# Longer lists of used rows in the second layer, and value rows copied next to their weights

## The chip, the cores and the metric

The kernel runs on one core of one Trainium2 chip. The metric is the device time of one execution in microseconds. Three runs of the kernel before took 1823.28, 1824.83 and 1824.98 us; the median is 1824.83 us. The change is judged by its median against that one.

## The reference

A decoder trunk of two layers over 256 tokens with 1024 features. Layer 0 mixes tokens by a state-space scan, layer 1 by causal attention. Behind each stands a product-key expert mixer (PEER), a layer norm, and a gated embedding. The change is in the expert mixer of layer 1:

```python
def block(xb):                                    # 128 tokens
    q = (xb @ w_q).reshape(128, 8, 2, 128)
    s = einsum('thcd,hcnd->thcn', q, sub_keys)
    v1, i1 = top_k(s[:, :, 0], 16)
    v2, i2 = top_k(s[:, :, 1], 16)
    cand = v1[..., :, None] + v2[..., None, :]
    best, pos = top_k(cand, 16)                   # 16 of 256 for each of 8 heads
    expert = take(i1 * 128 + i2, pos)
    gate = softmax(best)
    act = gelu(einsum('td,thkd->thk', xb, u[expert]))
    return einsum('thk,thkd->td', gate * act, v[expert])
```

There are 16384 experts, each with a row of u and a row of v (1024 floats). A token uses 8 x 16 of them.

## The kernel before

**Tiling.** The 256 tokens are two blocks of 128. The experts are 128 columns of 128 rows: row p of column e is expert 128 e + p. `peer(i)` does the expert mixer of layer i in four steps.

1. Queries, scores and the top-k lists ("route"), from lines 782 and 867 on.
2. `expert_in(e)` computes all 128 columns' products with u, whether used or not: 16 matmuls a column, accumulated in f32 from a high and a low part. Between the columns, `pick`, `spread` and `finish` make the gate of every (expert, token) and multiply it in. At the end `act[:, e, :]` holds the weight of every row of column e for all 256 tokens (columns from `MANY` = 92 on are in `high`). A matmul in line 993 counts beside it, per block of tokens, which rows of the first `MANY` columns are used at all.
3. `listing()` makes lists from that. A row of the first 92 columns that both token blocks use is of class "both"; one that only the first or the second uses is "one" or "two". Each class has places for `CAPS` = (37, 22, 22) groups of 128 rows, `GROUPS` = 81 in all. Prefix sums (`sums`, `ranks`), a 0/1 matrix per 8 columns (`place`) and a sort by `max` and `match_replace` (`order`) yield, for group s, the 128 row numbers: `picked["v"]` into v, `picked["w"]` into the table of weights. If a class overflows, a general loop over all columns runs behind a branch; else it is jumped over.
4. The sum over v. The last 36 columns are "dense": `expert_load` loads the 128 rows of v with SP and `expert_out` does 12 matmuls. The 92 others are done by groups: the weights were written to the DRAM tables `w_d` (256 tokens) and `a_d` (the first 128) by `keep` on ACT's DMA queue, 8 columns and 128 tokens a time. `fetched(s)` lets POOL (GpSimd) gather for a group first its 128 rows of weights, then its 128 rows of v. `group_load` splits both into a high and a low part (ACT casts, DVE subtracts), and `group_out` does 12 matmuls for "both" and 6 for the other classes.

**Order.** Engines work in order, and the code writes the order out by hand: `emit` sorts steps by a fraction of the stretch. Behind the last `expert_in` come six dense columns (`LEAD`), then the "one" groups with 13 dense columns between them (`MIX`), then the "both" and "two" groups (called inner) with the other dense columns but three and the loads of the gate's weights (`gate_load`). The last three dense columns (`LATER`) and the last two groups (`TAIL`) stand at the end, around the final layer norm. `issue_after` marks tie a step's instructions to the ones of the step before.

**Buffers.** In the "one" stretch, of three groups two gather v into the tiles `early` and one into the ring `raw` of four, which dense columns use too. In the inner stretch six tiles `raws` are used in turn. Split values go to the ring `hl` of four.

## Time and profile before

| what | us or count |
|---|---|
| profiled execution | 1825.7 |
| its span (first to last instruction) | 1823.9 |
| median of the runs | 1824.83 |
| second layer: attention and its start | about 929 to 1072 |
| second layer: queries and scores | about 1072 to 1131 |
| second layer: expert columns, gating | about 1131 to 1498 |
| second layer: lists built | about 1498 to 1532 |
| second layer: "one" groups | about 1532 to 1602 (POOL) |
| second layer: inner groups | about 1602 to 1784 |
| gathers in the second layer (L1189) | 162, 1531.88 to 1777.35 |

How to read it: the profile's first part gives the busy time and number of instructions of each engine; PE is the matrix engine, PEld its weight loads. In the second part each digit is the busy share in one of 40 slices of 45.6 us. In a table of stretches every engine has its busy time and number of instructions, then come the granted clock of PE, the share of the 16 DMA engines and GB/s. A row of the time order has the start, the duration and, in brackets, the idle time ahead with what ended it. `acc` are the sums, `hl` a split chunk, `w` a split weight tile.

### The profile page before, as it was taken

To read this page: it belongs to the slowest core of one execution; us is meant where nothing else is said; L and a number is where in the kernel's file an instruction comes from. 1 tells how busy PE (TensorE), PEld (TensorE's weight loads), DVE (VectorE), ACT (ScalarE), POOL (GpSimd) and SP (SyncE) were. 2 spreads that over 40 slices of the span, in tenths; PEclk is the share of its full clock that TensorE was granted. 3 is DMA by queue.
4 is the path that set the end of the run, shared out by engine and by line. 5 is a ranking of instruction groups with operands and counts; after the bars stand their busy time and mean duration, and the time that the engine had idled before them with its cause. 6 is when DMAs were issued, how large, how long until landed. Compare 5 with 4: busy or idle time off the path is not lost.

```text
span 1823.9 us, 31779 instructions
## 1 busy us (share of the span) xinstructions
PE 1806.1 (99%) x11152; PEld 1543.8 (85%) x11152; DVE 1493.5 (82%) x2948; ACT 1155.7 (63%) x2326; POOL 629.4 (35%) x608
## 2 busy tenths in 40 slices
PE   8999999999999999999999999999999999999999
PEld 7998888888888888788888788888888888887887
DVE  7798789988988997666667878998898899776675
ACT  6865556697665766565646655669666666665563
POOL 0011003332222247777700000333222224777770
PEclk9999999999999999999999999999999999999999
DMA  7655669898799998988836656989879999898880
GB/s 249 221 188 183 215 177 227 222 230 216 185 253 323 280 328 301 316 308 305 286 132 192 198 195 177 228 218 233 214 180 259 327 268 331 303 319 286 313 298 34
DMA packets 214890, 443.17 MB, mean 243 GB/s; under 512 B 18916, under 2 KB 123528, under 8 KB 213064
## 3 DMA queue, kind: packets, MB, share of 16 engines
q1 hardware_dynamic: 76360, 270.94, 45.7%
q0 software_dynamic: 66560, 133.99, 28.1%
q10 hardware_dynamic: 71808, 36.18, 6.9%
q8 instruction: 88, 1.44, 0.3%
q14 instruction: 74, 0.61, 0.1%
HBM read 364.98 MB, written 42.50 MB: 223 GB/s over the span
## 4 chain that ended last, share of the span: by engine, by line
PE 46%; DVE 4%; issue 3%; POOL 2%; ACT 2%; DMA 1%; POOLq 0%; DVEq 0%; ACTq 0%
PE acc L152 18%; PE acc L168 17%; PE acc L156 5%; PE mm L168 2%; POOL raw L1189 1%; DVE hl L127 1%; PE aux L992 1%; DMA raw<-in_v,r 1%; POOL rows_w L1189 1%; ACT hl L126 1%; PE mm L993 1%; PE mm L992 1%; PE aux L800 0%; DMA raw<-in_u 0%; DVE high L836 0%
## 5 line engine op out<-in xcount | busy, mean ns | idle before, releaser
L127 DVE TENSOR_TENSOR hl<-raw,hl 128x1024 fp32r<-128x1024 f32 x574 | 699.3, 1221 | 197.0 <-ACT hl L126 190.5
L168 PE MATMUL acc<-xT,hl 128*128 128x256 f32 (+1 forms) x4608 | 841.0, 340 | 1.5 <-DVE xT L195 0.8
L168 PEld LDWEIGHTS acc<-xT,hl 128*128 128x128 f32 x4608 | 701.1, 188 | 101.2 <-DVE hl L127 4.1
L126 ACT CAST hl<-raw 128x1024 fp32r<-128x1024 f32 x574 | 602.1, 1052 | 210.8 <-DMA raw<-in_v,r 105.3
L152 PE MATMUL acc<-hl,w 128*128 128x512 f32 x2196 | 502.2, 390 | 3.5 <-ACT hl L126 2.4
L152 PEld LDWEIGHTS acc<-hl,w 128*128 128x128 f32 x2196 | 412.5, 188 | 92.4 <-ACT hl L126 3.8
L932 POOL DMA_DIRECT2D w<-w x160 | 139.1, 869 | 400.1 <-ACT w L951 247.5
L932 POOL DMA_DIRECT2D act<-w x96 | 83.6, 871 | 302.8 <-ACT w L931 181.8
L1189 POOL DMA_INDIRECT raw<-in_v,r x132 | 153.4, 1162 | 40.2 <-issue 32.6
L930 ACT COPY w<-acc 128x256 f32<-128x256 f32 x160 | 59.8, 374 | 164.8 <-PE acc L168 159.7
L1189 POOL DMA_INDIRECT rows_w<-w_d,r x118 | 141.7, 1201 | 36.0 <-issue 32.0
L156 PE MATMUL mm<-xT,hl 128*128 128x256 f32 x816 | 100.9, 284 | 1.8 <-ACT hl L126 1.1
L156 PEld LDWEIGHTS mm<-xT,hl 128*128 128x128 f32 x816 | 98.6, 192 | 3.3 <-ACT hl L126 1.6
L931 ACT COPY w<-acc 128x256 f32<-128x256 f32 x256 | 97.3, 380 | 0.0
L930 ACT COPY act<-acc 128x256 f32<-128x256 f32 x96 | 35.7, 372 | 68.5 <-PE acc L168 68.1
L976 DVE TENSOR_TENSOR pick<-pick,r 128x2048 f16<-128x2048 f16 x64 | 78.2, 1222 | 0.9
L992 PEld LDWEIGHTS <-pick 128*128 128x128 f16 x1024 | 66.7, 98 | 14.3 <-issue 11.3
L221 POOL TENSOR_TENSOR ln_s<-ln_s,mhalf 128x1 f32<-128x1 f32 x8 | 4.4, 550 | 185.7 <-PE acc L156 130.6
L993 PE MATMUL mm<-pick 128*128 128x92 f16 x512 | 68.1, 204 | 0.0
L543 POOL TENSOR_TENSOR sq<-sq,sqt 128x256 f32<-128x256 f32 x12 | 12.5, 1040 | 150.2 <-ACT sqt L542 150.0
L992 PE MATMUL aux<-pick 128*128 128x128 f16 x688 | 59.6, 220 | 1.4 <-ACT high L1005 1.2
L1189 POOL DMA_INDIRECT pick<-a_d,r x44 | 52.2, 1187 | 14.9 <-issue 11.6
(298 smaller groups left out, 2133.2 us busy)
## 6 DMA issues: line engine op xcount, KB each, us to landing
raw<-in_u SPq DMA_DIRECT2D x256, 512.0 KB, 4.7
raw<-in_v SPq DMA_DIRECT2D x72, 512.0 KB, 5.3
w_d<-act ACTq DMA_DIRECT2D x44, 512.0 KB, 7.3
w<-w POOLq DMA_DIRECT2D x160, 128.0 KB, 5.6
raw<-in_w_q SPq DMA_DIRECT2D x32, 512.0 KB, 3.8
raw<-in_w_xbc SPq DMA_DIRECT2D x24, 512.0 KB, 4.1
act<-w POOLq DMA_DIRECT2D x96, 128.0 KB, 5.3
a_d<-act ACTq DMA_DIRECT2D x22, 512.0 KB, 10.2
```

The lines of the kernel that those rows point to most:

```text
L126: a = self.nc.scalar.copy(hi, src)
L127: b = self.nc.vector.tensor_tensor(lo, src, hi.bitcast(F32), op=OP.subtract)
L152: self.last_mm = self.nc.tensor.matmul(out, lhs(a), rhs(b), start=start and i == 0, stop=stop(n) and i == 2).ins
L156: self.last_mm = self.nc.tensor.matmul(out, lhs(a), rhs(b), start=start and i == 0, stop=stop and i == 2).ins
L168: self.nc.tensor.matmul(dst, hl[:, a, k * P:(k + 1) * P], src, start=k + a == 0, stop=(k, a) == order[-1] and k == KD - 1)
L930: nc.scalar.copy(whole, pe[:, :T])
L931: copied = nc.scalar.copy(pair[:, 1, :], pe[:, T:]).ins
L932: nc.gpsimd.dma_start(whole, pair[:, 1, :], accum_op=OP.add)
L976: nc.vector.tensor_tensor(a2, both, gates, op=OP.mult)
L992: nc.tensor.matmul(pg[:, t, :], one[:, 0, 4 * h + t], a2[:, 4 * h + t, k], start=k == 0, stop=k == 1)
L993: nc.tensor.matmul(banks["used"][:, MANY * tb:MANY * tb + MANY], one[:, 0, 4 * h + t], a2[:, 4 * h + t, 0, :MANY], start=at == 0, stop=at ...
L1189: got = nc.gpsimd.indirect_dma_start(out=dst, out_offset=None, in_=src, in_offset=rows(which))
```

## The change

In layer 1 alone the lists cover 104 columns instead of 92, and the places are 42, 25 and 25 groups. 40 of the 104 columns (the first ones) are staged: in the table `w_d` of that layer their rows are 1280 floats wide, 1024 for the row of v and 256 for the weights. While attention runs, ACT's queue copies v's rows there from DRAM to DRAM, one column a copy, paced by the chunks that are loaded; `keep` later writes the weights beside them. The lists are made so that the first 15, 8 and 8 groups of the classes take rows of the staged columns only, and such a group is gathered with one DMA of 1280 floats a row. The rest follows from the numbers: 24 columns stay dense, scores live in `act` instead of `high`, a fourth gate chunk is loaded early, and the last group's split goes to two buffers of the `raw` ring, in both layers.

```diff
-MANY = 92
-CAPS = (37, 22, 22)
+PLANS = ((92, 0, (37, 22, 22), (0, 0, 0)), (104, 40, (42, 25, 25), (15, 8, 8)))
+WIDE = D // T + 1
...
+    def staged(self, i):
+        return self.w_d[i][:(PLANS[i][1] * P + 1) * WIDE].rearrange("(n f) t -> n (f t)", f=WIDE)
+
+    def stage(self, i, c):
+        self.nc.scalar.dma_start(self.staged(i)[1 + c * P:1 + c * P + P, :D], self.dram["v"][i, c])
+
+    def spare(self):
+        self.chunks += 1
+        while self.copies and self.chunks * self.per_copy >= self.copied + 1:
+            self.copied += 1
+            with self.after(self.pace.marks):
+                self.copies.pop(0)()
...
             self.pace.marks = (dma.ins, hi, lo)
+        self.spare()
...
                 def places():
                     r = picked["ranks"]
+                    if STAGED:
+                        for k in range(3):
+                            V.tensor_scalar(short[:, k:k + 1], picked["total"][:, k:k + 1], -1.0, float(FIXED[k] * P),
+                                            op0=OP.mult, op1=OP.add)
+                        V.tensor_scalar(short, short, 0.0, None, op0=OP.max)
+                        V.tensor_tensor(r[:, :, STAGED:], r[:, :, STAGED:],
+                                        short[:, :, None].to_broadcast([P, 3, MANY - STAGED]), op=OP.add)
...
+                    for hi, at, n in ((STAGED, 0, f), (MANY, f, CAPS[k] - f)):
+                        src = key[:, k, :hi]
+                        for j in range(0, n, 8):
+                            top = best[k][:, at + j:at + j + 8]
+                            V.max(top, src)
...
+                full = s - BASES[kind] < FIXED[kind]
...
+                if full:
+                    at = D + (P if kind == 2 else 0)
+                    some, parts = home[:, at:at + t], ((home[:, :D + T], staged, "w"),)
...
-            last, two = two[-TAIL:], two[:-TAIL]
+            one = [s for k in range(len(one)) for s in (one_s[k // 2:k // 2 + 1] if k % 2 == 0 else []) + one[k:k + 1]]
+            ends = two_s or two
+            last = ends[-TAIL:]
...
+            pair = tuple(self.stream.tile([P, 1024], F32R, tag="raw", bufs=4, name=self.name("hl")) for _ in range(2))
+            end = [group_load(s, pair if k else None) for k, s in enumerate(last)]
...
     def run(self):
+        self.staging(0, 24, 46)
         self.ssd()
         self.peer(0)
+        self.staging(1, 2, 44)
         self.moba()
         self.peer(1)
```

POOL in the second layer's inner stretch, before (`rows_w` are gathered weights, `raw` gathered rows of v, `r` holds the row numbers):

```order
L1189 DMA rows_w_17921<-w_d_74,r_2042_16676 128x256
L1189 DMA raw_17919<-in_v,r_2042_16676 128x1024
L1189 DMA rows_w_17921<-w_d_74,r_2042_16676 128x128
L1189 DMA raw_17920<-in_v,r_2042_16676 128x1024
L1189 DMA rows_w_17921<-w_d_74,r_2042_16676 128x256
L1189 DMA raw_17915<-in_v,r_2042_16676 128x1024
```

The same place after, from the second half of a group on:

```order
L1249 DMA raw_18032<-in_v,r_2044_16723 128x1024
L1249 DMA raw_18033<-w_d_74,r_2044_16723 128x1280
L1249 DMA rows_w_18036<-w_d_74,r_2044_16723 128x256
L1249 DMA raw_18034<-in_v,r_2044_16723 128x1024
L1249 DMA raw_18035<-w_d_74,r_2044_16723 128x1280
L1249 DMA rows_w_18036<-w_d_74,r_2044_16723 128x128
L1249 DMA raw_18030<-in_v,r_2044_16723 128x1024
L1249 DMA rows_w_18036<-w_d_74,r_2044_16723 128x256
```

Six rows were three groups; of the eight rows, the two with 1280 are a whole group each.

POOL at the first "one" groups, before (`pick` are the two tiles `early`, the row with `w` is the last sum of a u column):

```order
L1189 DMA pick_17333<-a_d_76,r_2042_16676 128x128
L1189 DMA pick_17333<-in_v,r_2042_16676 128x1024
L932 DMA w_17176<-w_17176 128x256
L1189 DMA pick_17333<-a_d_76,r_2042_16676 128x128
L1189 DMA pick_17334<-in_v,r_2042_16676 128x1024
```

And after:

```order
L960 DMA w_17244<-w_17244 128x256
L1249 DMA pick_17412<-w_d_74,r_2044_16723 128x1280
L1249 DMA pick_17413<-a_d_76,r_2044_16723 128x128
L1249 DMA pick_17413<-in_v,r_2044_16723 128x1024
L1249 DMA pick_17413<-a_d_76,r_2044_16723 128x128
L1249 DMA raw_17462<-in_v,r_2044_16723 128x1024
```

The first gather now stands behind the last sum, and one group in three of this stretch is a wide one until the eight are used.

ACT during attention, after (`low` and `pt` are copies out of PSUM, `at` a split of attention's output):

```order
L129 DMA w_d_74<-in_v 128x1024
L144 CAST hl_10975<-raw_10974 128x1024
L144 CAST at_10781<-aux_10887 128x128
L144 CAST at_10781<-aux_10888 128x128
L129 DMA w_d_74<-in_v 128x1024
L637 COPY low_10931<-mm_10856 128x256
L144 CAST hl_11038<-raw_11037 128x1024
```

The two rows of L129 are copies; before, ACT issued no DMA here. 40 of them stand between the third chunk of attention and the thirteenth query chunk or so.

More of the change, by code (lines that the diff above doesn't have):

```diff
@@ L123, in raw, with staging @@
         return self.stream.tile([P, 1024], F32, tag="raw", bufs=4, name=self.name("raw"))
+    def staged(self, i):
[8 more added lines that the diff above has]
+                self.copies.pop(0)()
+    def staging(self, i, first, chunks):
+        n = PLANS[i][1]
+        self.copies = [lambda c=c: self.stage(i, c) for c in range(n)]
+        self.chunks, self.copied, self.per_copy = -first, 0, n / chunks
     def split(self, hi, lo, src):
@@ L1064, in listing @@
                 flag = picked["flag"] = take(2, 2, dt=U32)
-                wide = [-(-n // 8) * 8 for n in CAPS]
+                wide = [a - (a - n) // 8 * 8 for a, n in zip(FIXED, CAPS)]
+                short = take(1, 3, dt=F32)
                 best = [take(2, n, dt=F32) for n in wide]
@@ L1134, in order @@
                 def order(k):
[L1135 to L1140 removed]
+                    f = FIXED[k]
+                    for hi, at, n in ((STAGED, 0, f), (MANY, f, CAPS[k] - f)):
[3 more added lines that the diff above has]
+                            V.max(top, src)
+                            if hi == STAGED or j + 8 < n:
+                                if hi == STAGED and n - j < 8:
+                                    V.memset(top[:, n - j:], 3e38)
+                                V.match_replace(out=src, in_to_replace=top, in_values=src, imm_value=-3e38)
                 def rows(k):
                     s = slice(BASES[k], BASES[k] + CAPS[k])
+                    fixed, free = slice(s.start, s.start + FIXED[k]), slice(s.start + FIXED[k], s.stop)
                     b = best[k][:, :CAPS[k]]
@@ L1248, in peer @@
             stages = [[classes], [*sums, ranks], [], [places, ones[0]], ones[1:3], ones[3:5], ones[5:7], ones[7:9], ones[9:11],
-                      [ones[11], surplus], [keys, one], [], [two], [both]]
+                      [*ones[11:], surplus], [keys, one], [], [two], [both]]
             assert kept[0] == MANY
@@ L1272, in peer @@
             assert not lates
-            both, one, two = ([b + k for k in range(n)] for b, n in zip(BASES, CAPS))
-            last, two = two[-TAIL:], two[:-TAIL]
+            (both_s, both), (one_s, one), (two_s, two) = ((list(range(b, b + f)), list(range(b + f, b + n)))
+                                                         for b, f, n in zip(BASES, FIXED, CAPS))
+            one = [s for k in range(len(one)) for s in (one_s[k // 2:k // 2 + 1] if k % 2 == 0 else []) + one[k:k + 1]]
+            assert len(one) == CAPS[1]
+            ends = two_s or two
+            last = ends[-TAIL:]
+            del ends[-TAIL:]
             early = [tl([P, 1536], F32, "pick", 2) for _ in range(2)]
-            picked["n"], picked["order"], picked["split"] = -1, (), ()
+            picked["n"], picked["m"], picked["order"], picked["split"] = -1, -1, (), ()
             def extra(f):
@@ L1287, in emit @@
                     f(s)
-            inner = sorted(spread_over(group, both) + spread_over(group, two), key=lambda step: step[0])
+            inner = sorted(sum((spread_over(group, l) for l in (both_s, both, two_s, two)), []), key=lambda step: step[0])
             emit(spread_over(group, one), spread_over(dense, range(MANY + LEAD, MANY + LEAD + MIX)),
@@ L1315, in peer @@
             halves = [(later[:, k], self.chunk(dram["v"][i, P - LATER + k])) for k in range(LATER)]
-            end = [group_load(s, (half, wide[1][:, 8]) if k else None) for k, s in enumerate(last)]
+            pair = tuple(self.stream.tile([P, 1024], F32R, tag="raw", bufs=4, name=self.name("hl")) for _ in range(2))
+            end = [group_load(s, pair if k else None) for k, s in enumerate(last)]
             for k, (w, hl) in enumerate(halves):
@@ L1319, in peer @@
             dump = tl([P, D], F32, "pick", 2)
-            gts = raws[:2]
+            gts = [raws[k][:, :D] for k in range(2)]
             self.layer_norm(0, accs[0], x, gb0, gb1, dump, pool)
```

98 lines of the change are left out of this document (60 added, 38 removed).

## The prediction

> **What bounds the kernel now.** I read the page first, then the busy time by stretches, then the time order of PE and POOL in the second layer's last 300 us, and last the waits there.
>
> ```profile
> span 1823.9 us, 31779 instructions
> PE 1806.1 (99%) x11152; PEld 1543.8 (85%) x11152; DVE 1493.5 (82%) x2948; ACT 1155.7 (63%) x2326; POOL 629.4 (35%) x608
> ...
> POOL 0011003332222247777700000333222224777770
> ```
>
> PE is busy for 99% of the span, so a matmul removed should be time removed. POOL's 35% hides two stretches at 0.7, one per layer; the change works in the second, slices 35 to 38.
>
> ```profile
> core 0: us, PE busy (x) PEld busy (x) DVE busy (x) ACT busy (x) POOL busy (x), PEclk, DMA share, GB/s
> 929.00:1072.00 143.00, 141.99 (x814) 114.81 (x813) 102.16 (x213) 85.14 (x181) 1.63 (x3) 1.00 0.51 169
> 1072.00:1131.00 59.00, 59.00 (x361) 52.33 (x362) 47.94 (x150) 29.02 (x56) 1.89 (x2) 1.00 0.66 205
> 1131.00:1202.00 71.00, 71.00 (x410) 61.94 (x409) 66.59 (x213) 45.95 (x81) 21.52 (x25) 1.00 0.90 226
> ...
> 1395.00:1498.00 103.00, 101.76 (x812) 88.94 (x811) 91.22 (x160) 66.27 (x188) 25.60 (x30) 1.00 1.06 296
> 1498.00:1532.00 34.00, 34.00 (x270) 29.00 (x270) 31.29 (x70) 20.95 (x46) 9.61 (x12) 1.00 1.11 322
> 1532.00:1602.00 70.00, 69.63 (x307) 57.27 (x306) 56.70 (x107) 47.44 (x78) 52.69 (x45) 1.00 0.92 306
> 1602.00:1771.00 169.00, 166.94 (x728) 137.40 (x728) 114.80 (x153) 100.28 (x153) 134.24 (x115) 0.99 0.88 306
> ```
>
> The rows are attention, the queries, expert columns, the later half of the gating, the building of the lists, the "one" groups, and the "both" and "two" groups (the inner stretch). The engine that matters beside PE is POOL, seen in its order of time:
>
> ```profile
> 1531.88 1.07 POOL L1189 DMA_INDIRECT pick<-a_d,r  x1 [0.93 <-DMA w_d<-act]
> ...
> 1602.85 1.05 POOL L1189 DMA_INDIRECT rows_w<-w_d,r  x1 [0.30 <-issue]
> ...
> 1676.84 0.94 POOL L1189 DMA_INDIRECT raw<-in_v,r  x1 [0.30 <-issue]
> ...
> 1686.01 1.98 POOL L1189 DMA_INDIRECT rows_w<-w_d,r  x1 [0.30 <-issue]
> ...
> 1773.41 1.45 POOL L1189 DMA_INDIRECT raw<-in_v,r  x1 [0.30 <-issue]
> ```
>
> From the first inner gather (1602.85) to the 114th (1773.41) stand 113 intervals: 170.56 / 113 = 1.509 us each, of which 0.30 is "issue" every time. In the inner stretch POOL waits for no buffer: it runs flat out. One gather takes 0.94 to 1.98 us, and why shows on DVE:
>
> ```profile
> 1681.81 1.29 DVE L127 TENSOR_TENSOR hl<-raw,hl 128x1024 fp32r<-128x1024 f32 x1 [6.09 <-ACT hl L126]
> ...
> 1685.96 1.22 DVE L127 TENSOR_TENSOR hl<-raw,hl 128x1024 fp32r<-128x1024 f32 x1
> ...
> 1687.29 1.21 DVE L127 TENSOR_TENSOR hl<-raw,hl 128x1024 fp32r<-128x1024 f32 x1
> ```
>
> The short gather at 1676.84 lies in 6.09 us in which DVE was idle, the long one at 1686.01 under two splits. PE at the same time:
>
> ```profile
> 1531.79 3.82 PE L152 MATMUL acc<-hl,w 128*128 128x512 f32 x16
> 1535.97 97.31 PE L152 MATMUL acc<-hl,w 128*128 128x512 f32 x428 [0.37 <-DVE w L127]
> 1633.42 46.49 PE L152 MATMUL acc<-hl,w 128*128 128x512 f32 x204
> 1681.83 102.58 PE L152 MATMUL acc<-hl,w 128*128 128x512 f32 x444 [1.91 <-ACT hl L126]
> 1784.24 8.32 PE L152 MATMUL acc<-hl,pick 128*128 128x512 f32 x36
> ```
>
> PE loses only 0.37 + 1.91 us. 1092 matmuls in 252.45 us less 2.28 is **0.229 us a matmul**. So PE sets the time, but POOL ends its inner gathers at 1774.86 and PE the groups at 1784.24, a lead of only 9.4 us, which must hold a landing, two splits and a group's matmuls. That it is thin already shows in the inner stretch's waits:
>
> ```profile
> ACT hl L126 <- DMA raw<-in_v,r: 39.7, 24, 5.8
> ACT hl L126 <- PE acc L152: 19.5, 16, 1.5
> ...
> PE acc L152 <- ACT hl L126: 1.9, 1, 1.9
> ```
>
> ACT waits twice as long for gathered rows as for buffers that PE holds.
>
> **The change part by part.** *Matmuls.* A dense column or a "both" group is 12 matmuls, a "one" or "two" group 6. Before: 36 and 37 of 12, 44 of 6: 1140. After: 24 and 42 of 12, 50 of 6: 1092. That is 48 x 0.229 = **11.0 us** off PE, if it is fed.
>
> *Gathers.* Before 81 groups x 2 = 162. After, 92 groups, of which 31 need one: 153. But where they lie decides. The "one" stretch goes from 44 to 42, while its PE work (with the six dense columns ahead of it) grows from 72 + 288 to 72 + 306 matmuls. The inner stretch goes from 114 gathers to 109 (21 groups with one, 44 with two; the last two groups have one each), while its PE work falls from 732 matmuls to 666. At 1.509 us POOL now needs 164.5 us for what PE does in 666 x 0.229 = 152.5. Before it was 172.0 against 167.6. **POOL becomes the bound of the inner stretch.**
>
> When may it start? In the "one" stretch POOL is held by buffers:
>
> ```profile
> POOL pick L1189 <- DVE w L127: 2.7, 3, 1.5
> POOL pick L1189 <- DVE hl L127: 2.7, 2, 1.9
> ```
>
> 44 gathers at 1.509 would be 66.4 us, and it took 71.0. The buffers are as many as before, so I let POOL's lead over PE stay, and its inner start moves with PE's: 18 matmuls, 4.1 us later. Then it ends 5 x 1.509 = 7.5 us sooner for that stretch: 4.1 - 7.5 = -3.4 us. PE follows by a lead that I keep at 9.4. So of the 11.0 us, 7.6 come back as waits for gathers: **-3.4**. If all of the lead but 8 us can be used up (5.7 for a landing, the last row below, and 2.3 for the two splits of a group), it is -4.8.
>
> *Cost of a wide gather.* The trace has none of 5 KB rows. The nearest rows:
>
> ```profile
> L1189 POOL DMA_INDIRECT raw<-in_v,r x57 | 68.0, 1193 | 17.4 <-issue 13.7 <-DMA raw<-in_v,r 1.8 <-DVE hl L127 1.2
> L1189 POOL DMA_INDIRECT rows_w<-w_d,r x57 | 66.3, 1163 | 17.4 <-issue 15.2 <-DMA raw<-in_v,r 2.1
> ...
> raw<-in_v,r POOLq DMA_INDIRECT x57, 5.7
> ```
>
> 4 KB rows cost 1193 ns and rows of 1 KB or less 1163: it goes by the 128 rows, not their bytes. I take 1.2 us for 5 KB, as both rows have it; the ends are 0.94 (the short gather above) and 2.4, as two gathers.
>
> *Attention and queries.* 40 copies of 512 KB, DRAM to DRAM, issued on ACT's queue. ACT is busy 85.14 of 143 us there, and the slack hides the issuing. The copies share the DMA engines with SP's loads:
>
> ```profile
> q1 hardware_dynamic: 10855, 35.88, 54.5%
> ...
> raw<-in_w_qk SPq DMA_DIRECT2D x16, 512.0 KB, 4.5
> ...
> 998.06 3.10 PE L168 MATMUL mm<-xT,hl 128*128 128x512 f32 x16
> ```
>
> The first is for 929 to 1131 us: 35.88 MB in 0.545 x 202 = 110 us of all engines, 3.07 us per MB. If a copied byte costs what a loaded one does, 20.97 MB are 64 us, in 92 us left free. PE's work hides this: a load lands in 4.5 us, a chunk is 3.1 us of matmuls, and four raw buffers hold 12 us of them. Without that cover each late load would cost what it is late. I take +0.5, ends 0 and +12 (a third of the 36 us below).
>
> *Gating and lists.* The usage matmul grows from 92 to 104 columns, 256 times in stretches where PE hardly waits:
>
> ```profile
> 1292.69 0.20 PE L993 MATMUL mm<-pick 128*128 128x92 f16 x1
> ...
> 1292.85 0.37 PE L993 MATMUL mm<-pick 128*128 128x92 f16 x5
> ```
>
> Four more take 0.17 us, 42 ns per 92 columns; twelve more columns are 5.5 ns, x 256 = **+1.4**. DVE, busy 31.29 of 34 us while the lists are built, gets more there:
>
> ```profile
> L1112 DVE TENSOR_TENSOR pick<-iota,pick 128x1024 f16<-128x1024 f16 x11 | 7.2, 687 | 0.4 <-PE aux L1115 0.3
> ...
> L1138 DVE MAX8 r<-r 128x8 f32<-128x92 f32 x4 | 1.0, 254 | 0.0
> ```
>
> Twelve columns of ranks are 1.5 x 0.687 = 1.0 us; five small instructions for the short counts, at about 0.2, 1.0; one more maximum and replacement 0.5; rows longer by 13% some 0.5: 3 us. The first gather then starts some 3 us later, which the buffer waits of the "one" stretch swallow (4.6 us); for PE's own splits I take +0.5, ends 0 and +3. The kept weights grow by 13%, beside a DMA share of 1.06:
>
> ```profile
> q10 hardware_dynamic: 71808, 36.18, 6.9%
> ```
>
> 6.9% of 1824 us are 126, half of it in this layer, and 13% of that 8 us of all engines, under PE's work: +0.5, ends 0 and +4.
>
> *Layer ends.* The last group's split goes to two raw buffers instead of two tiles of its own. In layer 0 the next layer's value loads wait for it, behind them nothing on SP before the stores of x; their splits wait for the second norm anyway. 0, ends 0 and +1. The first layer's lists, groups and gathers are the same.
>
> **Sum:** -3.4 + 0.5 + 1.4 + 0.5 + 0.5 = -0.5 us. The profiled execution took 1825.7 us (span 1823.9), 0.9 over the median; 1824.83 - 0.5 = **1824.3 us**.
>
> **The rivals.**
> *PE stays the bound.* For it: gathers took 0.94 us where DVE let POOL alone, and at 0.94 + 0.30 the 109 need 135 us, under PE's 152. It decides from about 1.4 us each. Against: DVE's work per gather hardly changes. Then -11.0 + 2.9, and the 1.9 us wait gone: -10.0, 1815. DMA would carry in 152 us what takes 169 now at 306 GB/s, so 340, which no row here reaches (322 at most). The Trainium skill, page "DMA: Bandwidth & Descriptors", section "Anatomy of one DMA — SWDGE (gpsimd) path", would end here: it calls descriptor generation small and lays most of a DMA's fixed 2 us on the write's receipt, so that POOL would bound nothing. The trace differs: POOL is held 1.16 to 1.19 us by each gather, and 0.30 more.
>
> *The wide gather costs more (slower).* POOL may write more descriptors per row. 21 lie in the inner stretch, so each 0.1 us is 2.1 us: from +0.20 us it is slower than before by 0.2%. At 1.3 times: 21 x 0.36 = +7.6, 1832; as two gathers with an issue each, 21 x 1.509 = +31.7, 1856. For it: no row over 4 KB was ever gathered here. The Trainium skill, same page, section "SWDGE vs HWDGE vs iDMA", prefers packets of at most 4096 bytes, which a 5 KB row crosses. No run here shows a wider one. Against: 512 bytes, 1 KB and 4 KB all cost the same.
>
> *The copies crowd the loads (slower).* If a copied byte takes twice a loaded one's engine time, 110 + 128 us don't fit in 202, and 36 us spill into the expert columns, where the share is 0.90 already. It decides from 92 / 64 = 1.4 times. A third of the spill on PE, +12: 1836.
>
> *The lists overflow*, so that the general loop runs over all columns: over 450 us, 104 columns in turn at 4.5 us or more for a load. Counted on the reference's inputs, the second layer's lists hold 5205, 3030 and 3071 rows for 5376, 3200 and 3200 places: 0.01.
>
> **How the numbers follow.** Forecast 0.50 (own range 1820 to 1828), PE-bound 0.21, wide gather 0.15, copies 0.13, overflow 0.01. The range leaves out the dearer halves of the two slower ones and the PE-bound one's lowest tail: 1814 to 1834. A measurement of this kernel can tell about 0.2%, 3.6 us, from no change. Faster: 0.21 and 0.06 of the forecast; slower: 0.11 + 0.08 + 0.01 and 0.06; same: the rest.
>
> **What would show it.** Right: L152 has 48 matmuls fewer, and its rows break into many pieces with waits for ACT or DVE hl, some 8 to 10 us in all, in the inner stretch; POOL there has no gap but 0.30 and 109 gathers at 1.5 us. Wrong: wide gathers well off 1.2 us; PE unbroken to the end; PE waiting for raw loads in attention; a first gather later than PE's sixth dense column.

## The result and the profile after

The changed kernel took **1840.76 us** (median of six runs, 1836.72 to 1849.08); the kernel before took 1824.90 beside it (six runs, 1819.46 to 1826.69). The ratio is **1.0099, 95% interval 1.0071 to 1.0127**: 16 us slower by the medians, where 0.5 us faster was forecast. The profiled execution is the shortest of the six, 1836.72 us (span 1834.9), 11.0 over the profiled one of before. So the stages below account for 11.0 us, and the other five executions lost 1.3 to 12.4 us more.

The page of after, part 1 and the row of POOL in part 2:

```profile
span 1834.9 us, 31756 instructions
PE 1805.7 (98%) x11117; PEld 1532.8 (84%) x11117; DVE 1495.2 (81%) x2960; ACT 1152.9 (63%) x2336; POOL 617.3 (34%) x599
...
POOL 0011003332222247877600000333222224677780
```

PE and POOL had fewer instructions, as the change says (POOL's row counts 599 for 608), but PE's busy time is almost the same (1805.7 for 1806.1) and the span grew by 11.0: the time is in waits. PE's order of time finds them (start, duration, instruction, count, idle time ahead and what ended it):

```profile
975.78 8.63 PE L187 MATMUL mm<-xT,hl 128*128 128x512 f32 x48
...
1076.69 11.86 PE L187 MATMUL acc<-xT,hl 128*128 128x512 f32 x64
...
1497.97 0.21 PE L1021 MATMUL mm<-pick 128*128 128x104 f16 x1
...
1538.51 70.89 PE L171 MATMUL acc<-hl,w 128*128 128x512 f32 x306
1610.35 11.53 PE L171 MATMUL acc<-hl,w 128*128 128x512 f32 x48 [0.95 <-ACT hl L144]
1623.47 6.31 PE L171 MATMUL acc<-hl,w 128*128 128x512 f32 x24 [1.59 <-ACT hl L144]
1631.21 5.06 PE L171 MATMUL acc<-hl,w 128*128 128x512 f32 x18 [1.43 <-ACT hl L144]
1637.38 27.19 PE L171 MATMUL acc<-hl,w 128*128 128x512 f32 x114 [1.12 <-ACT hl L144]
1666.92 14.98 PE L171 MATMUL acc<-hl,w 128*128 128x512 f32 x62 [2.35 <-ACT hl L144]
...
1795.13 8.32 PE L171 MATMUL acc<-hl,pick 128*128 128x512 f32 x36
```

Such starts divide an execution into stages that can be compared between kernels: the first layer up to its last dense columns, the layer's end, attention (first k and q matmuls to the first query matmul), queries to the last usage matmul, lists (to the first dense matmul), the **tail** (first dense matmul to the 36 matmuls of the last three dense columns), and the end. Of before, the same rows start at 916.13, 974.48, 1071.83, 1491.70, 1531.79 and 1784.24.

| stage, us | before | after | difference |
|---|---|---|---|
| first layer | 916.13 | 917.49 | +1.4 |
| its end | 58.35 | 58.29 | -0.1 |
| attention | 97.35 | 100.91 | **+3.6** |
| queries, gating | 419.87 | 421.28 | +1.4 |
| lists | 40.09 | 40.54 | +0.4 |
| tail | 252.45 | 256.62 | **+4.2** |
| end | 39.66 | 39.77 | +0.1 |

In the tail PE has 48 matmuls fewer, 1044, which at 0.229 us are 239.1; it took 256.6, so it lost 17.5 us where it had lost 2.3. Of the 17.5, 11.3 are idle time of PE (245.3 us busy); the rest lies inside rows that count as busy, with the clock granted at 1.00. What fed it, POOL's gathers by form over the tail (count, busy us, mean ns, then idle time ahead with what ended it):

```profile
L1249 POOL DMA_INDIRECT raw<-in_v,r x52 | 64.1, 1232 | 17.5 <-issue 12.4 <-DVE hl L145 2.3 <-DMA rows_w<-w_d,r 1.2
L1249 POOL DMA_INDIRECT rows_w<-w_d,r x44 | 54.5, 1239 | 14.3 <-issue 11.9 <-DMA rows_w<-w_d,r 1.5 <-DMA raw<-in_v,r 0.9
L1249 POOL DMA_INDIRECT raw<-w_d,r x23 | 25.6, 1111 | 7.1 <-issue 5.9 <-DMA rows_w<-w_d,r 0.6 <-DMA raw<-in_v,r 0.3
L1249 POOL DMA_INDIRECT pick<-a_d,r x17 | 19.6, 1154 | 5.2 <-issue 5.2
L1249 POOL DMA_INDIRECT pick<-in_v,r x9 | 9.9, 1102 | 6.0 <-DVE hl L145 2.4 <-DVE r L1200 1.8 <-issue 1.2
L1249 POOL DMA_INDIRECT pick<-w_d,r x8 | 8.9, 1109 | 17.3 <-DVE w L145 7.9 <-DVE hl L145 5.0 <-DVE r L1180 4.3
```

These are the 153 gathers that were counted. The 31 wide ones (the rows that read `w_d` into `raw` or `pick`) took 1.11 us each, no more than the others. In the inner stretch POOL's gaps are 0.30 each but for four of 0.44 to 1.71; the eight wide gathers of the "one" stretch waited 17.3 us, 12.9 of it for their buffers (the rows of DVE `w` and `hl`) and 4.3 for the row numbers `r`.

And attention, all engines in order of time, with two rows of the list of DMA issues (issue, count, KB, median us to landing):

```profile
984.23 0.33 SPq L257 DMA_DIRECT2D raw<-in_pT  x1
...
990.24 0.62 ACT L144 CAST pT<-raw 128x512 fp32r<-128x512 f32 x1 [4.47 <-DMA raw<-in_pT]
990.77 0.36 ACT L637 COPY low<-mm 128x256 f32<-128x256 f32 x1
...
991.16 0.42 DVE L638 TENSOR_TENSOR k<-mm,low 128x256 f32<-128x256 f32 x1 [2.13 <-ACT low L637]
...
991.64 0.93 PE L686 MATMUL aux<-k,q 64*128 64x128 f32 x8 [1.94 <-DVE k L638]
```

```profile
w_d<-in_v ACTq DMA_DIRECT2D x40, 512.0 KB, 6.6
...
raw<-in_w_qk SPq DMA_DIRECT2D x16, 512.0 KB, 6.6
```

Beside the copies a load of `w_qk` lands in 6.6 us (4.5 before). The load of `pT` is the one that hurts: ACT stands 4.47 us in front of it, and the copy of `low`, which has nothing to do with it, is behind it in ACT's order; `k` waits for `low`, PE for `k`. PE falls 1.96 us behind the kernel before at this place and the other 1.6 us at short waits for `k` and `lg` (attention's scores) behind it. Before, the same wait of ACT was short:

```profile
985.53 0.62 ACT L126 CAST pT<-raw 128x512 fp32r<-128x512 f32 x1 [1.06 <-DMA raw<-in_pT]
```

### The profile page after: what moved, and what is told of

Its sections match the earlier page's. It is cut to its first block, busy times and chain, and to the rows that moved or that the text cites. A ratio compares the mean times of both kernels' runs of the same rounds, so it can differ in the third digit from the quotient of the medians.

```text
span 1834.9 us, 31756 instructions
## 1 busy us (share of the span) xinstructions
PE 1805.7 (98%) x11117; PEld 1532.8 (84%) x11117; DVE 1495.2 (81%) x2960; ACT 1152.9 (63%) x2336; POOL 617.3 (34%) x599
## 3 DMA queue, kind: packets, MB, share of 16 engines
q10 hardware_dynamic: 82224, 59.51, 10.6%
## 4 chain that ended last, share of the span: by engine, by line
PE 37%; DMA 7%; DVE 5%; issue 4%; POOL 3%; ACT 2%; ACTq 0%; POOLq 0%; DVEq 0%
PE acc L187 17%; PE acc L171 10%; PE acc L175 5%; DMA rows_w<-w_d,r 2%; DMA raw<-in_v,r 2%; DVE hl L145 2%; POOL raw L1249 2%; PE aux L1020 1%; ACT hl L144 1%; POOL rows_w L1249 1%; PE mm L187 1%; DMA raw<-in_w_qk 1%; DMA raw<-w_d,r 1%; PE mm L1021 1%; POOL pick L1249 1%
## 5 line engine op out<-in xcount | busy, mean ns | idle before, releaser
L171 PEld LDWEIGHTS acc<-hl,w 128*128 128x128 f32 x2160 | 401.5, 188 | 112.1 <-ACT hl L144 19.6
L1249 POOL DMA_INDIRECT raw<-in_v,r x118 | 139.1, 1179 | 37.6 <-issue 26.2
L1249 POOL DMA_INDIRECT rows_w<-w_d,r x103 | 122.6, 1190 | 32.2 <-issue 28.3
L1021 PE MATMUL mm<-pick 128*128 128x92 f16 (+1 forms) x512 | 68.6, 207 | 0.0
L999 DVE TENSOR_TENSOR pick<-iota,r 128x1024 f16<-128x1024 f16 x64 | 43.8, 685 | 11.6 <-PE aux L1020 5.4
```

The costliest lines, as they stand in the source:

```text
L171: self.last_mm = self.nc.tensor.matmul(out, lhs(a), rhs(b), start=start and i == 0, stop=stop(n) and i == 2).ins
L1021: nc.tensor.matmul(banks["used"][:, MANY * tb:MANY * tb + MANY], one[:, 0, 4 * h + t], a2[:, 4 * h + t, 0, :MANY], start=at == 0, stop=at ...
L1249: got = nc.gpsimd.indirect_dma_start(out=dst, out_offset=None, in_=src, in_offset=rows(which))
```

## The experiments

Eighteen runs were made in five sets (two of them with the kernels unchanged), each set on one chip, with runs of the kernel before beside it. That kernel took 1854 us in the first set, 1824, 1824 and 1826 in the next three, and 1847 in the last; in the first and the last, the first layer's tail, which the change leaves alone, was 259 to 270 us long, in the others 250 to 255 (260 once). Sets 4 and 5 ran on the same chip, so the chip alone does not explain the difference; its cause stays open. So ratios hold within a set; across sets I compare stages, and only where they repeat. "inner" counts the gathers from the inner stretch on, "first" is the first layer up to its last dense columns.

| set, kernel | ratio [95%] | first | its end | attention | tail | columns | inner |
|---|---|---|---|---|---|---|---|
| 1 e2 copies first | 1.0042 [1.0021, 1.0064] | 950.0 | 58.3 | 97.4 | 258.1 | 104 | 111 |
| 1 e3 unstaged | 1.0197 [1.0169, 1.0225] | 932.4 | 58.3 | 97.4 | 298.0 | 104 | 134 |
| 1 e4 one double | 1.0020 [0.9985, 1.0055] | 931.0 | 58.3 | 101.7 | 264.5 | 104 | 111 |
| 1 e5 lists 92 | 0.9953 [0.9930, 0.9976] | 930.9 | 58.3 | 101.7 | 250.8 | 92 | 95 |
| 2 e6 after again | 1.0085 [1.0059, 1.0110] | 917.5 | 58.3 | 98.9 | 259.9 | 104 | 111 |
| 2 e7 LEAD 8 | 1.0103 [1.0071, 1.0134] | 917.5 | 58.3 | 101.6 | 273.1 | 104 | 111 |
| 2 e8 staged 56 | 1.0104 [1.0080, 1.0128] | 934.6 | 58.3 | 102.4 | 250.6 | 104 | 101 |
| 2 e9 before again | one run, 1829.5 us | 918.1 | 58.8 | 97.4 | 255.7 | 92 | 118 |
| 3 e10 copies apart | 1.0157 [1.0134, 1.0180] | 933.8 | 58.3 | 97.8 | 271.5 | 104 | 111 |
| 3 e11 staged 88 | 1.0298 [1.0282, 1.0314] | 931.2 | 58.3 | 121.3 | 253.7 | 104 | 80 |
| 3 e12 lists 96 | 1.0078 [1.0060, 1.0095] | 931.6 | 58.3 | 97.3 | 243.3 | 96 | 93 |
| 3 e13 lists 92 | 1.0101 [1.0087, 1.0115] | 935.1 | 58.3 | 97.8 | 248.9 | 92 | 95 |
| 4 e14 copies apart, held | 1.0120 [1.0092, 1.0147] | 915.2 | 66.7 | 97.8 | 265.4 | 104 | 111 |
| 4 e15 lists 96, held | 1.0035 [1.0020, 1.0050] | 927.7 | 68.9 | 97.3 | 250.3 | 96 | 93 |
| 4 e16 lists 100, held | 1.0084 [1.0065, 1.0102] | 916.6 | 66.8 | 97.5 | 246.7 | 100 | 95 |
| 4 e17 lists 92, held | 1.0053 [1.0034, 1.0072] | 917.1 | 70.9 | 97.8 | 249.9 | 92 | 95 |
| 5 e18 lists 96, spread | **0.9955 [0.9926, 0.9984]** | 924.2 | 58.3 | 99.3 | 245.7 | 96 | 93 |
| 5 e19 spread | 1.0028 [1.0000, 1.0057] | 928.8 | 58.3 | 98.4 | 258.3 | 104 | 111 |

### Is it the kernel, or one execution? (e6, e9)

Both kernels unchanged, for a second pair of traces.

> The changed kernel as it is, for a second trace, beside a trace of the kernel before on the same chip. By stages, as in the first pair of traces: attention (its first k and q matmuls to the first query matmul) 3.5 to 4.5 us longer than before, queries and gating 1.4 longer, first dense matmul to the last groups 4 us longer; 1.009 of the time before. If the 4 us of the tail or of attention belong to one execution and not to the kernel, these differences change sign or go under 1 us.

> The kernel before, for a trace on the same chip as the others: stages to compare with. If this chip is one on which the first layer's gathers are starved too, its tail is well over 252 us and what the change does there differs from the first chip.

1.0085. Attention +1.5, queries and gating +4.2, tail +4.2 against e9, but e9's one run is 6 us over its kernel's median of 1823.6. The signs repeat, the sizes scatter by a few microseconds, as the executions do.

### Do gathers set the tail? (e3, e4, e7)

```diff
 e3
-PLANS = (..., (104, 40, (42, 25, 25), (15, 8, 8)))
+PLANS = (..., (104, 0, (42, 25, 25), (0, 0, 0)))
 e4
+PLANS = (..., (104, 40, (42, 25, 25), (15, 0, 8)))
 e7
+        LEAD, MIX = ((6, 13), (8, 11))[i]
```

> Lists of 104 columns as in the changed kernel, but no column is staged: no copies, and all 92 groups take two gathers, 184 in place of 153. Theory A (a gather that is saved saves only its own 0.94 + 0.30 us, because the splits on DVE that hold POOL up stay as many; in the stretch of the one-sided groups the buffers set the pace, not the gathers): 23 more gathers in the inner stretch and the last groups at 1.24 us, less 4.2 us for the copies: 1840.8 + 28.5 - 4.2 = 1865. Rival B (time goes by the number of gathers at 1.51 us each): 31 x 1.51 - 4.2 = +42.6, 1883.

> The 8 staged groups among the one-sided ones are gathered in two again (50 gathers in that stretch in place of 42); the 15 and 8 staged ones of the inner stretch stay. Theory A (three row buffers in turn set the pace of that stretch, about 9.1 us for three groups, whatever the number of gathers): the time stays within 3 us of 1840.8. Rival B (the number of gathers sets it): 8 x 1.51 = +12 us, 1853.

> The changed kernel, but in the second layer 8 dense columns stand ahead of the one-sided groups in place of 6 (and 11 among them in place of 13), so that PE has 24 matmuls, 5.5 us, more to do between the end of the lists and the first group. Theory A (the first gather comes 3.6 us after the first dense matmul in place of 0.1, and this lateness is never made up): the waits in the one-sided stretch go, and the tail from the first dense matmul to the last groups, 256.6 us, loses 4 to 5 us. Rival B (the buffers cap POOL's lead, and the inner stretch sets the end through POOL's 111 gathers alone): the gathers start as early as before, so that the tail changes by under 1.5 us.

**e3**: its tail is 298.0 us, against 258.1 of e2 on the same chip, which has the same lists and matmuls: 39.8 us more, between A's 28.5 and B's 46.8. Ahead of the inner stretch 5.7 us of it are lost. From the first inner gather to the start of the last, POOL took 201.3 us for 134 gathers, in e2 167.9 for 111: 1.45 us for each of the 23 more, at nearly the same pace (1.51 and 1.53 us a gather). **e4**: eight more gathers in the "one" stretch leave its length alone (POOL's first gather to the inner stretch: 79.4 us, 78.9 in e2). So there the number of gathers is not the pace. Its inner stretch was longer than e2's, which the edit doesn't explain (tail 6.4 us over; the clock was granted at 0.50 for 17 us of it, for 7 in e2, which may be the reason but is not shown to be); its total can't be set against 1840.8, as its set has no run of the changed kernel. **e7**: 5.5 us more of PE's work ahead of the groups saved nothing; the median went from 1840.4 to 1844.7 with overlapping intervals. My theory that the 3.6 us by which the first gather came late were the loss fell. What the tail needs is not an earlier start.

The profiled execution of e7 has a long tail (273.1 us) and shows why starved tails also scatter. Its stretches (PE's busy time and count first, then PEld, DVE, ACT, POOL; the granted clock stands third from the end):

```profile
1755.00:1760.00 5.00, 5.00 (x24) 4.14 (x23) 3.90 (x5) 2.03 (x3) 4.11 (x3) 1.00 1.01 393
1760.00:1765.00 5.00, 2.03 (x9) 1.36 (x8) 2.04 (x3) 2.60 (x4) 4.06 (x4) 0.86 1.03 398
1765.00:1770.00 5.00, 5.00 (x13) 3.90 (x12) 4.70 (x7) 3.98 (x7) 3.78 (x5) 0.50 0.93 320
```

After a stretch with PE idle for 3 us of 5, the clock is granted at 0.50, and 13 matmuls run where 24 did: this wait cost PE about half of the next 5 us too. It also followed a shorter wait: in the kernel before, the 1.91 us ahead of 1681.83 were followed by 3.4 us at 0.50, while the 2.35 us ahead of 1666.92 in the changed kernel were followed by 1.00. The Trainium skill, page "TensorE: Matmul & The Clock Gate", part "The HAM clock gate", states that after an idle window of about 3.4 us the array runs at half clock until it was busy for such a window. The half clock agrees with this trace, the length does not: both waits were under 3.0 us.

### How few gathers are enough? (e8, e11, e12)

```diff
 e8
+PLANS = (..., (104, 56, (42, 25, 25), (21, 8, 12)))
 e11
+PLANS = (..., (104, 88, (42, 25, 25), (34, 8, 20)))
 e12
+PLANS = (..., (96, 48, (38, 22, 23), (19, 7, 10)))
 all three, after the last groups of layer 0
+            some_ahead()      # 16 (e8) or 20 copies of layer 1, 3 or 4 a step
```

> Lists of 104 columns, but 56 columns staged and 41 of the 92 groups gathered at once (21, 8 and 12): 143 gathers in place of 153. 16 of the 56 copies are issued at the end of the first layer, where DMA is 0.3 to 0.4 busy, the other 40 over attention and queries as in the changed kernel. Theory A (POOL's gathers bound the tail: 10 fewer in the inner stretch at 1.2 to 1.5 us): the tail falls from 256.6 to 242 to 246 us, and PE's 1044 matmuls at 0.229 us, 239, come into reach; with attention still 4 us over, the time is 1826 to 1830 where the changed kernel has 1841 (0.994 of it). Rival B (each wide gather costs POOL or the DMA engines as much as two, or the late lists set the end): no gain over the changed kernel, and copies at the end of the first layer make its last stage longer.

> Lists of 104 columns with 88 columns staged and 62 of 92 groups gathered at once (34, 8 and 20): 122 gathers, some 80 of them from the inner stretch on, where the changed kernel has 111. PE's work is the changed kernel's. Theory A (the number of POOL's gathers bounds the inner stretch): PE becomes the bound, and the tail from the first dense matmul to the last groups falls from 256.6 and 259.9 us to 240 to 244 (1044 matmuls at 0.229 are 239). Rival B (not POOL, but the landing of rows, the splits or the DMA engines bound the inner stretch): the tail stays at 250 or more, as it was with 101 gathers (250.6). 68 of the 88 copies now lie in attention and queries, which get 8 to 20 us longer, so the whole time says little here; the tail is what is read.

> A middle way: lists of 96 columns (38, 22 and 23 groups, 1110 matmuls, 30 fewer than before), 48 columns staged, 36 of 83 groups gathered at once (130 gathers, 93 of them from the inner stretch on), copies apart (20 at the end of the first layer, 28 in late attention and queries), and a ring of weight buffers of 7 places. Theory A (POOL bounds only while it has too many gathers): PE is the bound, the tail is 1062 x 0.229 = 243.2 and 1 to 3 us of waits, 6 to 8 us under that of before; attention and usage cost 1 to 3 us: 0.996 to 0.999 of the time before. Rival B (something else in the tail bounds): tail at 250 or more, and the time not under that of before.

The early copies did not land where I meant them. Nothing tied them to the steps around, and the scheduler issued them among the first loads of the program; `first` is 14 to 18 us longer than in e6 in all kernels with that edit (e8, e10 to e13), and the totals forecast for e8, e10, e12 and e13 were all missed. So the totals of these say little, the stages do.

**e8**, 101 gathers: tail 250.6, 6 to 9 us less for ten gathers, but 11.5 above PE's 239.1; I had 242 to 246. **e11**, 80 gathers:

```profile
1583.13 12.99 PE L171 MATMUL acc<-hl,w 128*128 128x512 f32 x56 [0.21 <-DVE w L145]
1599.89 18.33 PE L171 MATMUL acc<-hl,w 128*128 128x512 f32 x72 [3.77 <-ACT hl L144]
1620.56 49.53 PE L171 MATMUL acc<-hl,w 128*128 128x512 f32 x210 [2.33 <-ACT hl L144]
1672.27 11.99 PE L171 MATMUL acc<-hl,w 128*128 128x512 f32 x42 [2.18 <-ACT hl L144]
1685.26 147.61 PE L171 MATMUL acc<-hl,w 128*128 128x512 f32 x648 [1.00 <-ACT hl L144]
```

All its waits are early: the first gather came 14.8 us after the first dense matmul, behind a wait of 12.79 us for the row numbers, whose sorted list of staged columns is longer here. From 1685 on PE runs 648 matmuls in one piece, 0.228 us each, on the same matmuls for which the changed kernel starved. **e12**, 93 gathers for 1062 matmuls (243.2 us at 0.229):

```profile
1554.88 239.40 PE L171 MATMUL acc<-hl,w 128*128 128x512 f32 x1046 [0.20 <-DVE w L145]
```

One piece from the first groups to the last: tail 243.3, as forecast. Now POOL is the one that waits, for buffers and some 24 us beyond its 0.30 a gather in the inner stretch, where it waited 2.6 us in the changed kernel. Neither landing times, nor splits, nor the DMA engines stand in the way of PE; the number of gathers beside its matmuls does.

### Does fewer gathers help with the old lists? (e5, e13, e17)

```diff
+PLANS = (..., (92, 40, (37, 22, 22), (15, 7, 8)))
+            slots_w = 7 if STAGED else 8           # also in e12, e15, e16 and e18
+            rows_w = new([P, slots_w, T], "rows_w") # e13 and e17 with the copies of e10 and e14
```

> Lists of 92 columns as before the change (37, 22 and 22 groups, 1140 matmuls), with the 40 copies and 30 of the 81 groups gathered at once; a ring of weight buffers has 7 places in place of 8 for room. PE does what it did before the change, and 132 gathers stand in place of 162. Theory A (PE bounds the kernel before; the copies cost 4.2 us in attention): 1824.9 + 4.2 - 1.9 (the one wait of the tail goes) = 1827. Rival B (the copies cost nothing): 1823. Rival C (POOL's gathers already bound the kernel before): well under 1815.

> Lists of 92 columns as before the change, 40 columns staged, 30 of 81 groups gathered at once (132 gathers), copies apart as in the first kernel of this set. PE does what it did before the change. Theory A (PE bounds the kernel before on this chip): tail 250 to 252 us, attention 0 to 1 us longer, 0.999 to 1.001 of the time before. Rival B (POOL's 162 gathers cost the kernel before time in most of its executions, the profiled one being a good one): 0.997 or less.

> Lists of 92 columns, 40 staged, 132 gathers, 1140 matmuls as before the change, with the early copies held in place. PE's tail is 1092 x 0.229 = 250 us, as before. Theory A: tail 249 to 251, attention and the end of the first layer 0 to 2 us: 0.999 to 1.001 of the time before. If it is 0.997 or less, POOL's gathers cost the kernel before time in its ordinary executions; if 1.002 or more, the copies cost more than the stages show.

Tails of 250.8, 248.9 and 249.9, PE waiting 0.4 to 1.1 us of them: 1092 matmuls are 250.1. So with 118 inner gathers the kernel before (252.5, 255.7) stands just at the edge. e5 gains, 0.47% by the ratio, although its attention is 4 us longer; that the kernel before lost this in its tail in set 1 is not shown, as no trace of it was taken there. e13 and e17 lose by their copies: their totals were forecast at 0.999 to 1.001, and against the first profile of before `first` is 19 us longer in e13 and the layer's end 12.6 in e17, while the other stages change by under 4 us.

### What do the copies cost, and where? (e2, e10, e14)

```diff
 e2
-        self.staging(0, 24, 46)
+        self.staging(1, 24, 46)      # layer 1's copies, in layer 0's front part
         self.ssd()
         self.peer(0)
-        self.staging(1, 2, 44)
 e10: 20 early ones as above, the others from
+        self.staging(1, 22, 24)
 e14: as e10, the early ones tied to the steps around
+            some_ahead(7, self.norm_marks[0])
...
+            some_ahead(7, self.norm_marks[1])
...
+            some_ahead(6, self.pace.marks)
```

> The 40 copies of the second layer's value rows are issued in the first layer's front part, between its 25th and 70th chunk of weights, and none during the second layer's attention; all else stays. Theory A (the copies make SP's loads late in attention, and PE waits there): the 4.2 us that PE lost in attention between its start and the queries go away, so 1840.8 becomes 1836.6; if the same bytes crowd the front part of the first layer (DMA share 0.61, PE without waits) some of it comes back there, 0 to 4 us. The tail from the first dense matmul to the last groups keeps its 256.6 us. Rival B (attention's waits come from something else, the copies cost nothing): 1840.8, and the waits for k and lg stay in attention.

> The changed kernel with its 40 copies moved out of attention's dense part: 20 at the end of the first layer, where DMA is 0.3 to 0.4 busy and PE waits for no load, 20 from the 24th chunk of the second layer on (late attention, queries). Theory A (copies beside the loads of w_qk made PE wait in attention): the stage from the first k and q matmuls to the queries goes from 99 to 102 us back to 97.4 to 98.4, the last stage of the first layer stays 58.3, and the time falls by 2 to 4 us under the changed kernel's 1840. Rival B (the cost is in the copies' number, wherever they are): the same microseconds come back in the queries or at the end of the first layer, and the time stays at 1840.

> The changed kernel with its 40 copies apart again, this time held in their place: 7 after each of the two norms at the end of the first layer and 6 after the next loads, 20 from the 24th chunk of the second layer on. In the last set the early copies had been put ahead of everything, among the first loads of the program, where the first layer's front part got 14 to 16 us longer. Theory A (copies cost what they delay of the loads beside them): the front part is as before, the end of the first layer and attention cost 0 to 1.5 us together, and the time falls from the changed kernel's 1840 by 2 to 4 us. Rival B (the 14 to 16 us at the front belong to something else that the edit moved): the front part stays long, 1855.

Without copies, attention is 97.4 us in every trace (before, e2, e3, e9); with 40 beside it, 98.9 to 102.4; with 20 late ones, 97.8; with 68 (e11), 121.3. That part of theory A holds. But no place was free. In e2 the first layer got about 18 us longer (950.0 against 931 to 932 on that chip), 14 of it ahead of its tail, where 0 to 4 had been forecast. In e14 the early copies were held in their place and `first` is as before (915.2), but the layer's end went from 58.3 to 66.7 where 0 to 1.5 us had been forecast, with DMA engines that were 0.44 busy there before. ACT's rows show where (ACTq are its DMA issues):

```profile
929.34 11.32 ACTq L129 DMA_DIRECT2D w_d<-in_v  x7
...
931.45 4.09 PE L175 MATMUL acc<-wide,xT 128*128 128x512 f32 x10 [2.73 <-DVE xT L214]
...
940.70 0.59 ACT L213 CAST xT<-mm 128x512 fp32r<-128x512 f32 x1 [11.27 <-DMA w_d<-in_v]
...
956.91 0.52 ACTq L129 DMA_DIRECT2D w_d<-in_v  x1
```

The view merges the seven into one row of 11.32 us. Asked for by itself, line 129 shows what an issue takes (duration min/median/max in ns; us to landing), and narrower windows show single issues out of the seven:

```profile
L129 ACTq DMA_DIRECT2D w_d<-in_v x40: 518/519/672, 920.9 to 1120.2; - x40
DMA to landing us min/median/max: 4.1/6.5/13.0
929.34 0.52 ACTq L129 DMA_DIRECT2D w_d<-in_v  x1
935.23 0.52 ACTq L129 DMA_DIRECT2D w_d<-in_v  x1
```

So the seven issues are some 4 us, and between them ACT stands, from 929.86 to 935.23 for one. By the trace's semaphore events the first of these two was released at 929.32, as a copy of the burst before it landed, the second at 935.21, as a load of `w_v` landed: the copies waited for earlier transfers, and the casts behind them in ACT's order waited too. Why a copy waits for such a transfer is not shown. The Trainium skill, page "DMA: Bandwidth & Descriptors", section "Issuing engines are not separate DMA queues", calls the issuing time usually small against the DMA; the trace agrees, with at most 0.67 us against 4.1 or more.

### A version that gains? (e15, e16, e18, e19)

e15 and e16 are lists of 96 and of 100 columns with copies as in e14. e18 and e19 issue no burst: chunk by chunk, 7 (4) copies up to the 20th chunk of the second layer, 26 (22) up to the 46th, 15 (14) between the 104th and 134th. They differ in the lists.

```diff
 e15
+PLANS = (..., (96, 48, (38, 22, 23), (19, 7, 10)))
 e16
+PLANS = (..., (100, 56, (40, 23, 24), (21, 7, 12)))
 e18, lists of e15; e19, lists of the changed kernel
+        self.turns_at = [int(a + (b - a) * k / m)
+                         for a, b, m in ((4, 20, 7), (20, 46, 26), (104, 134, 15)) for k in range(m)]
```

> Lists of 96 columns, 48 staged, 130 gathers, 1110 matmuls, as in the last set, with the 20 early copies held at the end of the first layer. Theory A (with 93 gathers for 1062 matmuls PE bounds the tail, which was 243.3 us): front part as before, tail 243 to 245, attention and usage 1 to 3 us: 1818 to 1822, 0.996 to 0.999 of the time before. Rival B (copies cost the same wherever they lie): 1830 or more.

> Lists of 100 columns (40, 23 and 24 groups, 1098 matmuls), 56 staged, 40 of 87 groups gathered at once: 134 gathers, 95 from the inner stretch on, copies 20 at the end of the first layer and 36 over attention and queries. PE's tail is 1050 x 0.229 = 240.4 us; 95 gathers at 1.5 us are 143, PE's inner work 678 x 0.229 = 155. Theory A (POOL bounds only when gathers x 1.5 come over PE's matmuls): tail 241 to 244, attention 2 to 4 us: 1818 to 1823. Rival B (the late lists of the longer list set the tail): 246 or more, 1825 or more.

> Lists of 96 columns, 48 staged, 130 gathers, 1110 matmuls (as in the runs with tails of 243.3 and 250.3 us), none of the copies in a burst: 7 between the 4th and 20th chunk of the second layer, 26 to the 46th (late attention and queries), 15 between the 104th and 134th (the early gating, DMA share 0.75). Theory A (copies cost by their rate against the loads beside them, gathers cost only when their number holds POOL behind PE): tail 243 to 246, all stages ahead of it 1 to 3 us over the kernel before: 0.996 to 0.999 of its time. Rival B (48 copies cost 8 us or more wherever they lie): 1.001 or more.

> The changed kernel's lists (104 columns, 40 staged, 153 gathers, 1092 matmuls) with its 40 copies spread in the same way: 4 to the 20th chunk, 22 to the 46th, 14 between the 104th and 134th. Theory A: attention falls to 97.5 to 98.5 us, nothing comes back elsewhere, but the tail stays at 256 to 272 because 111 gathers hold the inner stretch: 1834 to 1842, 1.005 to 1.010 of the time before. Rival B (the copies were the whole loss): 1.002 or less.

e15 and e16 missed: their tails are short (250.3, with one spell of low clock, and 246.7), though longer than forecast, the bursts at the layer's end cost 10.6 and 8.5 us, and e16 has 7.5 us more in queries and gating. **e18 is a little faster than the kernel before, 0.9955 [0.9926, 0.9984], and e19, with copies spread in the same way (40 for 48) on the same chip, is not: 1.0028**, which is also less than its forecast of 1.005 to 1.010. The medians, 1839.5 and 1850.7, are 11.1 us apart; the tails, 245.7 and 258.3, by 12.6. From 1647 on e18's PE has no wait (first fence), e19's is in pieces to the end (second):

```profile
1647.02 143.06 PE L172 MATMUL acc<-hl,w 128*128 128x512 f32 x630
```

```profile
1733.89 11.16 PE L172 MATMUL acc<-hl,w 128*128 128x512 f32 x48 [1.44 <-ACT hl L145]
1745.58 21.25 PE L172 MATMUL acc<-hl,w 128*128 128x512 f32 x90 [0.54 <-ACT hl L145]
1767.21 19.36 PE L172 MATMUL acc<-hl,w 128*128 128x512 f32 x84 [0.38 <-ACT hl L145]
```

The gain of e18 was measured where the kernel before took 1847 us. Against the first profile of before its stages give attention +2.0, queries and gating +1.9, lists +0.5, tail -6.7: 2.3 us less, which the measurement could not tell from nothing. That it gains in the conditions of the first measurement is not shown.

## Why the prediction was wrong

**The step that failed** is in "Gathers", on POOL: "its inner start moves with PE's: 18 matmuls, 4.1 us later. Then it ends 5 x 1.509 = 7.5 us sooner", hence -3.4. The bound was the right one, POOL; but it began later than counted and hardly got shorter, and the tail came out at +4.2 (profiled). POOL in the inner stretch by itself, before and after (busy us and count of each engine as above):

```profile
1602.85:1771.62 168.77, 166.71 (x728) 137.21 (x727) 114.57 (x153) 99.98 (x152) 134.31 (x114) 0.99 0.88 306
1619.01:1787.12 168.11, 158.00 (x670) 123.37 (x669) 110.33 (x147) 96.30 (x146) 132.58 (x109) 1.00 0.88 303
```

The first row also shows a misreading. The 114 gathers were over at 1771.62; the one at 1773.41, which the prediction took for the 114th, is the 116th, of the last two groups. So a gather took 167.61 / 113 = 1.483 us from start to start, not 1.509, and POOL's lead over PE was 12.6 us, not 9.4. The saving of five gathers stays about the same, 7.4. What the runs showed in place of the step:

- *Start of the inner stretch.* Measured from the first dense matmul, POOL began it at 71.1 us before and 80.5 after: 9.4 later, not 4.1. The row buffers set the pace of the "one" stretch, and they do it by groups (two rows of POOL's order of time after):

```profile
1553.40 1.05 POOL L1249 DMA_INDIRECT pick<-w_d,r  x1 [2.74 <-DVE r L1180]
...
1608.13 0.93 POOL L1249 DMA_INDIRECT pick<-w_d,r  x1 [1.34 <-DVE w L145]
```

  Between these two stand six rounds of three groups, 54.73 / 6 = 9.1 us a round (before, five rounds from 1541.05 to 1589.15, 9.6). The three more groups, 25 for 22, are one more round, 9.1 us. I had counted PE's matmuls there, and gathers, of which e4 showed that eight more cost nothing. The other traces agree in size: with 25 groups the inner stretch began at 80.2 to 88.1 us, with 22 at 71.1 to 75.1 (79.5 in e15).
- *Length of the inner stretch.* The 109 gathers took 168.1 us, from 1619.02 to 1787.12, where 114 had taken 168.8: 0.7 less, not 7.5. A gather held POOL 1.22 us for 1.18, 4.2 us in all, and POOL's four longer gaps add 2.6 us beyond 0.30 each, where it had none. Why a gather took longer stays open.
- *The lead at the end*, which the forecast kept, fell from 12.6 to 8.0, 4.6 us less. So the alternative was right here: the lead was used up down to its 8 us for a landing and two splits (7.9 to 10.1 in the other traces with 111 or 101 inner gathers).

Against the forecast these are +5.3, +6.8 and -4.6: together 7.5, but for rounding the distance from -3.4 to +4.2. What the sum could not show is the slope: between 134 and 111 inner gathers a gather is worth 1.45 us (e3, e2), between 111 and 101 still 0.6 to 0.9 of the tail (the changed kernel, e6, e8), and PE is in one piece only with 93 for 1062 matmuls (e12) or, once its lists are there, 80 for 1044 (e11).

**Copies**, +0.5 with an end at +12, measured +3.6 (1.6 to 4.4 in other traces with the same copies). The rate was right: from 929 to 1131 us the copies took 30.2% of the engines for 20.97 MB, 61 us against 64 counted. So the rival "if a copied byte takes twice" was wrong in its reason. The cover was wrong: four raw buffers hide late chunks, but `pT` is loaded just ahead of its use, and ACT's order lets everything behind wait. That wait grew by 3.4 us (1.06 to 4.47); 1.96 of attention's 3.6 us follow on it directly. Through the other traces attention grows with it: 97.3 to 97.8 us where the wait was 0.9 to 1.2, 98.4 at 1.4, 98.9 and 99.3 at 3.0, 100.9 to 102.4 at 4.3 to 5.5; e11, with 68 copies, has other waits.

**Right:** 153 gathers and 1092 matmuls; a wide gather at 1.2 us (1.11); the usage matmul, +1.4 (queries and gating +1.4, where the two traces of before differ by 1.9, so the exact match is luck); lists and kept weights +1.0 (+0.4); layer ends 0; PE in pieces with waits for ACT hl, 11.3 us idle for 8 to 10 forecast, POOL with hardly a gap but 0.30. The first gather came 3.5 us later against PE, as counted; that it cost nothing by itself is what e7 supports.

**The rivals.** "PE stays the bound" is out: e12 shows what that looks like. "The wide gather costs more" is out by 1.11 us. "Copies crowd the loads" is true in its direction, at a third of its price.

**The median** lies 4.0 above the profiled execution. That its tails scatter is seen (256.6 to 273.1 in eight traces with 111 inner gathers and 1044 matmuls, 248.9 to 250.8 in the three of 92 columns with 95), and the clock after waits is one reason in some (e7); how much of the 4.0 it is, stays open.

## What to carry to other kernels

Work taken off an engine is time only while whoever feeds it keeps up: here the inner stretch got 9% fewer matmuls (732 to 666) but only 4% fewer gathers (114 to 109), with the feeder already at its limit, and the trade turned only when gathers fell faster than matmuls. Count a stretch that waits for buffers in rounds of its ring, not in instructions. And spare bandwidth is not free: look for the one load that is issued just ahead of its use, and for what stands behind the engine that waits for it or that issues the copies.

## What the runs showed of the hardware

- In the changed kernel's tail an indirect gather of 128 rows held POOL 1.11 us with rows of 5 KB, 1.10 to 1.23 with 4 KB and 1.15 to 1.24 with 1 KB or less: bytes made it no dearer. The wide ones landed in 6.3 and 6.7 us, the others in 5.0 to 5.5.
- DRAM to DRAM copies took 2.9 us of all 16 engines per MB (61 us for 20.97 MB), as much as loads into SBUF beside them (50.8% of 202 us for 35.97 MB: 2.9).
- Issuing a DMA of 512 KB took ACT 0.52 to 0.67 us, also in a burst; seven in a row still held ACT for 11.3 us, as some waited for earlier transfers to land (e14).
- PE's clock was granted at 0.50 for 3.4 us after a wait of 1.91 us (before) and for about 6 us after one of 2.97 (e7), and stayed at 1.00 after one of 2.35 (the changed kernel).
